# High and low weight parts in turn: the order of matmuls in block products and memory projections

## The chip, the cores and the metric

The kernel runs on one core of a Trainium2 chip. The metric is the device time of one execution in microseconds. An execution is described by five engines that each take their instructions in the order of the program: TensorE (PE in the profile, its weight loads apart as PEld), VectorE (DVE), ScalarE (ACT), GpSimd (POOL) and SyncE (SP), which issues most DMAs.

## The reference

One layer of a hybrid encoder for 512 tokens of width 2048, in float32:

```
y  = xn @ w_in                      # one input projection, xn = RMSNorm(x)
h += concat[GDN(y), RWKV7(y)] @ w_out
h += CrossAttn(RMSNorm(h), RMSNorm(mem)) :
     q = hn @ wq ; k = mn @ wk ; v = mn @ wv     # 256 memory tokens, 4 heads
     p = softmax(q k^T * XA_HEAD_DIM ** -0.5) ; (p v) @ wo
h += square(relu(hn @ mlp_w_up)) @ mlp_w_down    # hidden width 8192
out = RMSNorm_final(h)
```

The weights and the vectors are float32. The products of the kernel work on parts in a shorter format: a value is split into a high part, which is the value rounded, and a low part, which is what the rounding left.

## The kernel before, in words

**Stages.** PE goes through the following stages: 0 to 926 us, input projections (`py`) with the two mixers between them; 926 to 1036, the memory's key projections (`kp`), among the last of the mixers' work; 1036 to 1125, `kq`, a product of the query weights with the keys; 1125 to 1217, the memory's value projections (`vp`); 1217 to 1302, `vo`; 1302 to 1460, the out-projection as block products (`op`); 1460 to 1639, attention; 1639 to 2277, the first MLP matrix as block products (`up`); 2277 to 2897, the second.

**High and low.** A block of weights of 128x1024 is loaded by DMA (tiles `wr`, `ua`, `ub`), ACT casts it to its high part `whi` (line 130, 1.05 us), and DVE subtracts to get the low part `wlo` (line 131, 1.22 us); `split` issues both. The activations are split too; a tile of 128x512 holds the high part in its first 256 columns (`HA`) and the low part in the other 256 (`HB`). So a matmul of `whi` with all 512 columns forms high x high and high x low, and a matmul of `wlo` with the first 256 columns forms low x high. Both add to the same PSUM bank.

**Block products.** `op` has 8 steps p and `up` has 32, each with seven products on 2x2 blocks: B11 to bank x, T1 to y, T2 added on x, B21 to z, T3 added on x, B22 added on y, T4 added on x. After B11, T2 and T3 the bank x is read before the next product adds to it: ACT copies 256 columns into a tile `sl` and DVE adds the other 256 (after T3, DVE alone adds both). The weights of T1 and T2 are sums (`s1`) that DVE forms; those of T3 and B22 are sums too. At p = 0 of each stage the products go through `block`, at the others through `wide` (lines 1314 to 1321): eight high matmuls over k = 0..7, then eight low ones. There are 7 x 7 + 31 x 7 = 266 wide products. The activations' tiles are `cb0` (B11), `cb1` (T1), `cb2` (T2), `cb3` (T3), `cb4` (T4), `cb5` (B22) and `cb6` (B21).

**Buffers.** `whi` and `wlo` rotate over three buffers each (two in one pool, one in another), one step per product. So the cast of a product waits until the product three places earlier has read its high part for the last time; the buffer of B22 is that of T2.

**Memory projections.** `kp` (lines 546 to 552) and `vp` (lines 1354 to 1365) add up 16 blocks k for each of 16 output blocks. Both take the low matmul of a block before its high one, except at the first block of an output (`vp`: of each half), which starts with the high one. `kq` takes high, then low, all through. In the profile, all operations of the planned region up to `kq` carry line 228, and those of `vp`, `vo` and attention line 122, those of the helpers that issue them.

**What sets the order.** Up to `kq` the order is that of a plan in the program, which steps through generators. Behind it the code is issued through a tile framework, whose scheduler puts the instructions of each engine into an order of its own; the order of the code is not kept where data do not force it. PE then takes its rows strictly in the order that results.

Of the kernel before, what the change touches and what calls it, by code (L numbers as in the profile page):

```python
# [19 lines left out]
M = 256  # L20
KD = 16
# [52 lines left out]
def build(tc, I, out):  # L74
# [43 lines left out]
    def psb(nm, tag="mx", bufs=2):  # L118
        return tile_of(ps, [P, 512], F32, tag, nm, bufs)

    def mm(o, l, r, start=True, stop=True):
        PE.matmul(o, l, r, start=start, stop=stop)  # L122
# [59 lines left out]
    DV, AC, GS, TE, SY = (Lane(e, k) for e, k in ((V, "DVE"), (S, "ACT"), (GP, "POOL"), (PE, "PE"), (nc.sync, "SP")))  # L182
# [67 lines left out]
    def chain(gen, rank, done=None):  # L250
        chains.append([gen, rank, done, None, None])

    def after(*ev):
        return lambda: ev in events
# [63 lines left out]
    def act_tile(nm, dt=F32R):  # L318
        return tile_of(pa, [P, 512], dt, "act", nm, 32)
# [101 lines left out]
    def half(i):  # L421
        return lambda: i in halves and (i not in piece or ("piece", i) in events)
# [57 lines left out]
    def evict(n, pt):  # L480
        yield after("rstd")
        yield lambda: bool(yfree)
        b = yfree.pop(0)
        if n == 2:
            y = ybuf[b][0:64, 3:515]
            yield AC.copy(y, pt[64:128, :])
            yield DV.tensor_tensor(out=y, in0=pt[0:64, :], in1=y, op=ALU.add)
            yield DV.tensor_tensor(out=y, in0=y, in1=rstd[0:64, :], op=ALU.mult)
        else:
            yield DV.tensor_tensor(out=ybuf[b][:, 3:515], in0=pt, in1=rstd, op=ALU.mult)  # L490
        ys[n] = b
        events.add(("py", n))

    def gemm_(pts, his, los, first, nk=KD, left=None):

        w = len(pts)
        for h in range(nk // 8):
            for j in range(w):
                yield half(first + h * w + j)
            for kk in range(8):  # L500
                k = h * 8 + kk
                sl = slice(kk * P, (kk + 1) * P)
                yield lambda: len(his) > k
                if kk == 4:
                    yield lambda: all(first + h * w + j in whole for j in range(w))
                for j, pt in enumerate(pts):
                    wh, wl = halves[first + h * w + j]
                    yield TE.matmul(pt, wh[:, sl], his[k], start=(k == 0), stop=False)
                    yield TE.matmul(pt, wh[:, sl], los[k], start=False, stop=first == 4 and k == nk - 1)
                    if first != 4:  # L510
                        yield TE.matmul(pt, wl[:, sl], his[k], start=False, stop=(k == nk - 1))
                if left:
                    events.add((left, k))
            for j in range(w):
                used.add(first + h * w + j)
# [3 lines left out]
    def projections():  # L519
        pts = [psb(f"py{n}") for n in range(2)]  # L520
        yield from gemm_(pts, xhi, xlo, 0)
        for n in range(2):
            chain(evict(n, pts[n]), 0)
        for n in range(2, NIN):
            if n == NSQ[3] + 3:
                yield after("macc")
                pt = psb("pms", "mm", 2)
                mc = ybuf[macc[0]]
                yield TE.matmul(pt[:, 0:M], ones, mc[:, 0:M], start=True, stop=False)
                yield TE.matmul(pt[:, 0:M], ones, mc[:, M:2 * M], start=False, stop=True)  # L530
                chain(memnorm(pt, mc[:, M:2 * M]), 1)
            if n >= 4:
                yield after("py", n - 2)
            pt = psb(f"py{n}", "mm", 2)
            yield from gemm_([pt], xhi, xlo, 2 * n, left="x" if n == NIN - 1 else None)
            chain(evict(n, pt), 0)
        yield after("py", NIN - 2)
        kpt = {}
        for i, (n, h) in enumerate(kpo):
            if h == 0:  # L540
                yield after("kr", n - 2) if n >= 2 else after("py", NIN - 1)
                kpt[n] = psb(f"kp{n}", "mm", 2)
            pt = kpt[n]
            yield half(NKP + i)
            wh, wl = halves[NKP + i]
            for k in range(8 * h, 8 * h + 8):
                yield lambda: len(mhl) > k
                sl = slice(k % 8 * P, k % 8 * P + P)
                ab = [TE.matmul(pt, wh[:, sl], mhl[k], start=k == 0, stop=k == KD - 1),
                      TE.matmul(pt[:, 0:M], wl[:, sl], mhl[k][:, 0:M], start=False, stop=False)]  # L550
                yield from (ab if k == 0 else ab[::-1])
            used.add(NKP + i)
            if h == 0:
                continue
            khl.append(act_tile(f"khl{n}"))
            chain(kevict(n, pt, khl[n][:, 0:M], khl[n][:, M:2 * M]), 0)
        for i in range(2 * KD):
            n, g = i // 2, i % 2
            yield after("kp", KD - 2 + i) if i < 2 else after("kq", i - 2)
            yield half(NKQ + i)  # L560
            wh, wl = halves[NKQ + i]
            if i == 0:
                yield after("gated")
            pts = [psb(f"kq{n}_{g}_{hh}", t, 2) for hh, t in enumerate(("mm", "mg"))]
            for hh, o in enumerate(pts):
                for d in range(4):
                    k = g * 8 + hh * 4 + d
                    sl = slice((hh * 4 + d) * P, (hh * 4 + d + 1) * P)
                    yield TE.matmul(o, wh[:, sl], khl[k], start=(d == 0), stop=False)
                    yield TE.matmul(o[:, 0:M], wl[:, sl], khl[k][:, 0:M], start=False, stop=(d == 3))  # L570
            used.add(NKQ + i)
            chain(qevict(i, pts), 0)
# [590 lines left out]
    mhl = []  # L1163
# [26 lines left out]
    def memnorm(pt, mw):  # L1190
        yield from rsq_(mw, pt[:, 0:M], 1.0 / 2048, b_eps6)
        events.add(("mrs",))
        yield lambda: all(("py", i) in events for i in range(NIN))
        yield AC.copy(mrs, mw)
        events.add(("mrs", 1))
# [38 lines left out]
    def hilo():  # L1234
        cnt[0] += 1
        return (third("whi", f"whi{cnt[0]}", F32R, pw, NWS, "split", 1), third("wlo", f"wlo{cnt[0]}", F32R, pw, NWS, "split", 0))
# [78 lines left out]
    def wide(pt, a, parts, start):  # L1315
        hi, lo = hilo()
        split(a, hi, lo)
        for k in range(8):
            PE.matmul(pt, hi[:, k * P:k * P + P], parts[k], start=start and k == 0, stop=False, skip_group_check=True)  # L1319
        for k in range(8):  # L1320
            PE.matmul(pt[:, HA], lo[:, k * P:k * P + P], parts[k][:, HA], start=False, stop=k == 7, skip_group_check=True)  # L1321

    def block_or_wide(p, pt, a, parts, start):
# [28 lines left out]
    for n2 in range(8):  # L1352
        hi, lo = act_tile(f"vhi{n2}"), act_tile(f"vlo{n2}")
        for i in range(2):
            n = 2 * n2 + i
            pt = psb(f"vp{n}", "mm", 2)
            for h in range(2):
                wh, wl = wload(I["wv"][n][:, h * 1024:(h + 1) * 1024])
                for k in range(h * 8, h * 8 + 8):
                    sl = slice(k % 8 * P, k % 8 * P + P)  # L1360
                    if k == 0:
                        mm(pt, wh[:, sl], mhl[k], start=True, stop=False)
                    mm(pt[:, 0:M], wl[:, sl], mhl[k][:, 0:M], start=False, stop=False)
                    if k > 0:
                        mm(pt, wh[:, sl], mhl[k], start=False, stop=k == KD - 1)
            h2, l2 = hi[:, i * M:(i + 1) * M], lo[:, i * M:(i + 1) * M]
            u, t = rstd[:, M:2 * M], sl2(M)
            S.copy(u, pt[:, M:2 * M])
            V.tensor_tensor(out=t, in0=pt[:, 0:M], in1=u, op=ALU.add)
            V.tensor_tensor(out=t, in0=t, in1=mrs, op=ALU.mult)  # L1370
            split(t, h2, l2)
            vhi.append(h2)
            vlo.append(l2)
            mixes(1 + n % 2)
    for h in range(4):
        for g in range(4):
            pts = [psb(f"vo{g}_{h}_{mt}", ("mm", "mg")[g % 2]) for mt in range(2)]
            for q in range(2):
                wh, wl = wload(I["wo"][g, h][:, q * 1024:(q + 1) * 1024])
                for mt in range(2):  # L1380
                    for e in range(2):
                        d = q * 2 + e
                        sl = slice(e * 512, e * 512 + 512)
# [119 lines left out]
    for g in range(2):  # L1503
        pts = [psb(f"sc{g}_{t}", *(("mm", 2), ("mm", 2), ("mg", 2), ("mg", 2), ("scr", 1), ("scg", 1), ("mm", 2), ("mm", 2))[4 * g + t]) for t in range(4)]
        for n2 in range(8):
# [4 lines left out]
            wh, wl = hilo()  # L1510
# [40 lines left out]
        if g == 1:  # L1551
            for n in (0, 1, 2):
                pt = psb(f"at{n}", "mg", 2) if n < 2 else psb(f"at{n}", "scr", 1)
                begun.append((pt, *wload(vo_of(n))))
                attend(*begun[n], range(4))
        for e in range(2):
            for mt in range(2):
                pt = psb(f"ptr{g}_{e}_{mt}")
# [92 lines left out]
    for n in range(KD):  # L1651
        if n < 3:
            pt = begun[n][0]
            attend(*begun[n], range(4, 8))
        else:
            pt = psb(f"at{n}", "mm", 2)
# [374 lines left out]
```

## Time and profile before

| | before |
|---|---|
| runs, median (lowest to highest) | 2899.75 us (2895.79 to 2900.2), 3 runs |
| the profiled execution's own time | 2898.35 us |
| its span in the trace | 2896.6 us |
| granted TensorE clock in it | 0.999 |

The span runs from the first to the last instruction in the trace; 1.75 us of the execution's time lie around it. The page has the busy time of each engine, a row of tenths over 40 slices of the span (72.4 us each), the chain of work that ended last, and groups of instructions. In the timeline, PE matmuls that follow one another are given as one row with a count, the time from the first start to the last end; the matmuls are pipelined, so that one of 128x512 has a duration of 0.39 us but the next starts 0.23 us behind it. In the chain a group of matmuls counts from start to the next start.

### The profile page before, as it was taken

What the parts mean: (1) busy time and instruction counts of PE and PEld (TensorE: products, weight loads), DVE (VectorE), ACT (ScalarE), POOL (GpSimd) and SP (SyncE); (2) the same over time, 40 slices, a digit from 0 to 9 for tenths busy, and PEclk for the clock granted to TensorE, in tenths of its full rate; (3) what the DMA queues carried; (4) which work ended last, traced back from release to release, by engine and by line L of the source; (5) the groups of instructions that cost most, each with busy time, mean ns of one, the idle gap of its engine ahead of it and who ended that gap; (6) DMA issues with size and microseconds to landing.
All of it is one profiled execution on the core that took longest, in us unless ns stands there. A gap on an engine that the chain in (4) does not pass through costs nothing.

```text
span 2896.6 us, 48156 instructions
## 1 busy us (share of the span) xinstructions
PE 2870.5 (99%) x18458; PEld 2408.6 (83%) x18458; DVE 2223.9 (77%) x3379; ACT 1561.9 (54%) x2256; POOL 310.2 (11%) x704
## 2 busy tenths in 40 slices
PE   9999999999999999999999999999999999999998
PEld 7787787887877888889888888888888878888887
DVE  7676676676676767769866898888998897878776
ACT  7544554554546555664455555555555655454444
POOL 0302213113113000001111100010010000000000
PEclk9999999999999999999999999999999999999999
DMA  5333333424334579797788767788777988776765
GB/s 193 100 89 85 99 90 86 105 69 100 105 98 137 159 243 298 267 308 199 205 218 209 195 194 219 229 234 248 214 206 207 288 261 278 221 261 209 255 191 178
DMA packets 304503, 546.64 MB, mean 189 GB/s; under 512 B 97224, under 2 KB 178380, under 8 KB 303248
## 3 DMA queue, kind: packets, MB, share of 16 engines
q1 hardware_dynamic: 245264, 449.17, 49.3%
q0 software_dynamic: 35840, 67.12, 11.6%
q10 hardware_dynamic: 23168, 27.27, 2.6%
q8 instruction: 145, 2.38, 0.3%
q14 instruction: 86, 0.70, 0.1%
HBM read 479.10 MB, written 131.48 MB: 211 GB/s over the span
## 4 chain that ended last, share of the span: by engine, by line
PE 92%; DVE 3%; DMA 2%; POOL 1%; issue 1%; ACT 1%; SPq 0%; ACTq 0%; POOLq 0%; DVEq 0%
PE py L228 20%; PE upx L1319 8%; PE upx L1321 4%; PE upy L1319 4%; PE dx L1786 4%; PE dx L1785 4%; PE dx L1788 4%; PE vp L122 3%; PE kq L228 3%; PE sc L122 3%; PE at L122 3%; PE kp L228 3%; PE vo L122 3%; PE upy L1321 2%; PE upz L1319 2%; PE opx L1319 2%
## 5 line engine op out<-in xcount | busy, mean ns | idle before, releaser
L130 ACT CAST whi<-ub 128x1024 fp32r<-128x1024 f32 x290 | 304.5, 1052 | 274.1 <-PE dy L1786 59.0
L131 DVE TENSOR_TENSOR wlo<-ub,whi 128x1024 fp32r<-128x1024 f32 x290 | 352.6, 1220 | 60.5 <-ACT whi L130 55.1
L228 PE MATMUL py<-xhi,whi 128*128 128x512 f32 x928 | 371.0, 400 | 6.3 <-ACT xhi L228 6.3
L228 PE MATMUL py<-xlo,whi 128*128 128x512 f32 x928 | 372.1, 401 | 0.0
L228 PE MATMUL py<-xhi,wlo 128*128 128x512 f32 x912 | 370.9, 407 | 0.0
L228 ACT CAST whi<-wraw 128x1024 fp32r<-128x1024 f32 (+1 forms) x180 | 187.3, 1041 | 260.9 <-PE py L228 162.1
L130 ACT CAST whi<-ua 128x1024 fp32r<-128x1024 f32 x205 | 215.5, 1051 | 191.3 <-PE dx L1786 62.3
L131 DVE TENSOR_TENSOR wlo<-ua,whi 128x1024 fp32r<-128x1024 f32 x205 | 249.7, 1220 | 52.6 <-ACT whi L130 51.8
L228 DVE TENSOR_TENSOR wlo<-wraw,whi 128x1024 fp32r<-128x1024 f32 (+1 forms) x178 | 223.2, 1254 | 70.5 <-ACT whi L228 68.1
L1319 PE MATMUL upx<-cb,whi 128*128 128x512 f32 x992 | 249.8, 394 | 0.7 <-DVE sl L1277 0.7
L228 PEld LDWEIGHTS py<-xhi,whi 128*128 128x128 f32 x928 | 175.3, 189 | 40.6 <-ACT xhi L228 6.6
L228 PEld LDWEIGHTS py<-xlo,whi 128*128 128x128 f32 x928 | 174.9, 189 | 38.3 <-DVE xlo L228 1.0
L1319 PEld LDWEIGHTS upx<-cb,whi 128*128 128x128 f32 x992 | 178.5, 189 | 33.0 <-DVE sl L1277 0.9
L228 PEld LDWEIGHTS py<-xhi,wlo 128*128 128x128 f32 x912 | 172.4, 189 | 32.7 <-issue 1.0
L1785 PE MATMUL dx<-whi,dh 128*128 128x512 f32 x480 | 186.7, 389 | 0.0
L1786 PE MATMUL dx<-whi,dl 128*128 128x512 f32 x480 | 186.7, 389 | 0.0
L1321 PEld LDWEIGHTS upx<-cb,wlo 128*128 128x128 f32 x992 | 135.3, 190 | 9.7
L1321 PE MATMUL upx<-cb,wlo 128*128 128x256 f32 x992 | 138.3, 282 | 0.0
L131 DVE TENSOR_TENSOR wlo<-wr,whi 128x1024 fp32r<-128x1024 f32 x80 | 97.7, 1223 | 43.5 <-ACT whi L130 42.4
L1788 PE MATMUL dx<-wlo,dh 128*128 128x512 f32 x480 | 128.6, 389 | 0.0
L228 ACT ACT_TABLE_LOAD x86 | 110.3, 1283 | 26.2 <-DVE suml_gn L228 11.6
L1319 PE MATMUL upy<-cb,whi 128*128 128x512 f32 x496 | 124.3, 392 | 0.0
(898 smaller groups left out, 6676.2 us busy)
## 6 DMA issues: line engine op xcount, KB each, us to landing
ws<-in_w_dn POOLq DMA_DIRECT2D x128, 512.0 KB, 7.2
wraw<-in_w_in SPq DMA_DIRECT2D x116, 512.0 KB, 3.8
ua<-in_w_dn SPq DMA_DIRECT2D x108, 512.0 KB, 4.5
ub<-in_w_up SPq DMA_DIRECT2D x71, 512.0 KB, 6.3
ua<-in_w_up SPq DMA_DIRECT2D x56, 512.0 KB, 4.7
ub<-in_w_dn SPq DMA_DIRECT2D x52, 512.0 KB, 4.7
sl<-cd SPq DMA_DIRECT2D x104, 256.0 KB, 5.0
ub<-ws SPq DMA_DIRECT2D x52, 512.0 KB, 4.2
```

The lines of the kernel that those rows point to most:

```text
L122: PE.matmul(o, l, r, start=start, stop=stop)
L130: tie(S.copy(hi, src))
L131: V.tensor_tensor(out=lo, in0=src, in1=hi.bitcast(F32), op=ALU.subtract)
L228: f(*a, **k)
L1319: PE.matmul(pt, hi[:, k * P:k * P + P], parts[k], start=start and k == 0, stop=False, skip_group_check=True)
L1321: PE.matmul(pt[:, HA], lo[:, k * P:k * P + P], parts[k][:, HA], start=False, stop=k == 7, skip_group_check=True)
L1785: PE.matmul(pts[t], uh[:, x], hi[:, w], start=start and z == 0 and q == 0, stop=False, skip_group_check=True)
L1786: PE.matmul(pts[t], ul[:, x], hi[:, w], start=False, stop=False, skip_group_check=True)
L1788: PE.matmul(pts[t], uh[:, x], lo[:, w], start=False, stop=z == 1 and q == 3, skip_group_check=True)
```

## The change

In three places the high and the low matmul of a block now follow one another: in `wide` one loop issues both for each k, and in `kp` and `vp` the high one always comes first. Number, shapes and operands of the matmuls are as before.

```diff
@@ kp, line 546 @@
             for k in range(8 * h, 8 * h + 8):
                 yield lambda: len(mhl) > k
                 sl = slice(k % 8 * P, k % 8 * P + P)
-                ab = [TE.matmul(pt, wh[:, sl], mhl[k], start=k == 0, stop=k == KD - 1),
-                      TE.matmul(pt[:, 0:M], wl[:, sl], mhl[k][:, 0:M], start=False, stop=False)]
-                yield from (ab if k == 0 else ab[::-1])
+                yield TE.matmul(pt, wh[:, sl], mhl[k], start=k == 0, stop=False)
+                yield TE.matmul(pt[:, 0:M], wl[:, sl], mhl[k][:, 0:M], start=False, stop=k == KD - 1)
@@ wide, line 1317 @@
         for k in range(8):
             PE.matmul(pt, hi[:, k * P:k * P + P], parts[k], start=start and k == 0, stop=False, skip_group_check=True)
-        for k in range(8):
             PE.matmul(pt[:, HA], lo[:, k * P:k * P + P], parts[k][:, HA], start=False, stop=k == 7, skip_group_check=True)
@@ vp, line 1358 @@
                 for k in range(h * 8, h * 8 + 8):
                     sl = slice(k % 8 * P, k % 8 * P + P)
-                    if k == 0:
-                        mm(pt, wh[:, sl], mhl[k], start=True, stop=False)
-                    mm(pt[:, 0:M], wl[:, sl], mhl[k][:, 0:M], start=False, stop=False)
-                    if k > 0:
-                        mm(pt, wh[:, sl], mhl[k], start=False, stop=k == KD - 1)
+                    mm(pt, wh[:, sl], mhl[k], start=k == 0, stop=False)
+                    mm(pt[:, 0:M], wl[:, sl], mhl[k][:, 0:M], start=False, stop=k == KD - 1)
```

What the scheduler makes of it, at p = 8 of `up`. The rows are line, operation, tile written, tiles read, and shape; the number behind `up` is p, that behind `cb` is the set and then k. The high matmul's line is 1319 before and 1318 after, the low one's 1321 and 1319.

PE before, at the end of T3 (`cb3`), where B22 (`cb5`) begins:

```order
L1321 MATMUL upx8_18888<-cb3_6_16550,wlo1039_18986 128x256
L1321 MATMUL upx8_18888<-cb3_7_17227,wlo1039_18986 128x256
L1319 MATMUL upy8_18889<-cb5_0_16558,whi1040_19007 128x512
L1319 MATMUL upy8_18889<-cb5_1_16559,whi1040_19007 128x512
L1319 MATMUL upy8_18889<-cb5_2_16560,whi1040_19007 128x512
L1319 MATMUL upy8_18889<-cb5_3_16561,whi1040_19007 128x512
```

PE after, at the end of B21 (`cb6`), which here stands before T3:

```order
L1318 MATMUL upz8_18890<-cb6_7_17230,whi1038_18962 128x512
L1319 MATMUL upz8_18890<-cb6_7_17230,wlo1038_18963 128x256
L1318 MATMUL upy8_18889<-cb5_0_16558,whi1040_19007 128x512
L1319 MATMUL upy8_18889<-cb5_0_16558,wlo1040_19008 128x256
L1318 MATMUL upy8_18889<-cb5_1_16559,whi1040_19007 128x512
L1319 MATMUL upy8_18889<-cb5_1_16559,wlo1040_19008 128x256
L1318 MATMUL upx8_18888<-cb3_0_16544,whi1039_18985 128x512
L1319 MATMUL upx8_18888<-cb3_0_16544,wlo1039_18986 128x256
```

Before, the products followed one another whole: T1, T2, B21, T3, B22, T4. After, eight matmuls of B21 stand before T2 and eight behind it, then four of B22, then T3, then B22's other twelve. The same pattern stands at p = 8, 11, 14, 15 and 18; at p = 22, 27, 28 and 29 it is nine and seven of B21. At the other p these products stay whole or are cut by one or two rows; where rows of B22 stand ahead of T3 there (p = 1, 4 and 25), fourteen or fifteen of B21 stand between T2 and them.

PE after, a little later, at the end of B22, where T4 (`cb4`) begins:

```order
L1318 MATMUL upy8_18889<-cb5_7_17229,whi1040_19007 128x512
L1319 MATMUL upy8_18889<-cb5_7_17229,wlo1040_19008 128x256
L1318 MATMUL upx9_19086<-cb0_0_16523,whi1044_19091 128x512
L1318 MATMUL upx8_18888<-cb4_0_16551,whi1041_19031 128x512
L1319 MATMUL upx8_18888<-cb4_0_16551,wlo1041_19032 128x256
```

The first high matmul of B11 of p = 9 (`upx9`) stands ahead of T4 of p = 8, and the rest of that B11 behind it. One to four rows of the next p's B11 stand there at 23 of the p. Before, that happened at p = 4, 10, 11, 17, 18, 24 and 31 alone, with one to three rows.

DVE before, ahead of T2 of p = 8, with B11's eviction `sl1033` as the last row (`wlo1037` is the low part for T2, `wlo1038` for B21):

```order
L1277 TENSOR_TENSOR sl1025_18694<-sl1025_18694,upx7_18690 128x256
L131 TENSOR_TENSOR wlo1037_18940<-ub85_18887,whi1037_18939 128x1024
L131 TENSOR_TENSOR wlo1038_18963<-ub84_18885,whi1038_18962 128x1024
L1274 TENSOR_TENSOR sl1024_18693<-sl1024_18693,sl1025_18694 128x256
L1277 TENSOR_TENSOR sl1033_18891<-sl1033_18891,upx8_18888 128x256
```

DVE after, at the same place:

```order
L131 TENSOR_TENSOR wlo1037_18940<-ub85_18887,whi1037_18939 128x1024
L1273 TENSOR_TENSOR sl1024_18693<-sl1024_18693,sl1025_18694 128x256
L1273 TENSOR_TENSOR tt7_18857<-sl1024_18693 128x256
L1273 TENSOR_TENSOR t4_7_18858<-sl1025_18694,tt7_18857 128x256
L131 TENSOR_TENSOR wlo1038_18963<-ub84_18885,whi1038_18962 128x1024
L1276 TENSOR_TENSOR ub84_18885<-ub84_18885,ub85_18887 128x1024
L1276 TENSOR_TENSOR sl1033_18891<-sl1033_18891,upx8_18888 128x256
```

B11's eviction moved behind the 128x1024 addition into `ub84`, which stood behind it before.

## The prediction

> **What bounds the kernel now.** I read the page first: the busy shares, and then the chain that ended last.
>
> ```profile
> PE 2870.5 (99%) x18458; PEld 2408.6 (83%) x18458; DVE 2223.9 (77%) x3379; ACT 1561.9 (54%) x2256; POOL 310.2 (11%) x704
> ...
> DVE  7676676676676767769866898888998897878776
> ...
> PE 92%; DVE 3%; DMA 2%; POOL 1%; issue 1%; ACT 1%; SPq 0%; ACTq 0%; POOLq 0%; DVEq 0%
> ```
>
> TensorE is busy for 99% of the span and carries 92% of the chain. So the time is decided by two things only: how fast PE steps from one matmul to the next, and whether it ever waits. In the stages that the change touches, the chain of waits (out-projection block products, 1323 to 1459 us; then a closer window) is a plain row of products without a gap:
>
> ```profile
> 1323.19 1.84 PE opx L1319 x8
> ...
> 1330.62 0.95 PE opx L1321 x8
> 1331.57 1.84 PE opz L1319 x8
> 1333.41 0.95 PE opz L1321 x8
> 1334.36 1.84 PE opx L1319 x8
> ...
> 1373.47 1.84 PE opx L1319 x8
> ```
>
> Eight high matmuls take 1.84 us, eight low ones 0.95 us. From the first row to the last lie 18 products, (1373.47 - 1323.19) / 18 = **2.793 us a product**, 349.2 ns for a high and low pair. The list of PE's waits from 1300 to 2290 us, which holds out-projection, attention and MLP up, says that almost nothing else happens there:
>
> ```profile
> PE upx L1310 <- ACT whi L130: 0.8, 1, 0.8
> PE upx L1319 <- DVE sl L1277: 0.7, 1, 0.7
> PE at L122 <- ACT phi L1562: 0.2, 1, 0.2
> ```
>
> The columns are the total, the number of waits and the longest: 1.7 us in all. A gain from removed waits is therefore not to be had in these stages. The change can win only by a faster step, and it can lose both by a slower step and by new waits.
>
> **The change, part by part.** Number and shapes of the matmuls, the casts, the subtractions and the DMAs stay. Only PE's order is written anew; the other engines' order follows from the scheduler.
>
> *1. The step of a pair in turn.* Two stages of before already alternate 128x512 high with 128x256 low matmuls, and the chain gives a row of each:
>
> ```profile
> 1036.24 87.95 PE kq L228 x507
> ...
> 1125.00 90.25 PE vp L122 x512
> ```
>
> `kq` takes high, low, high, low without a break: 87.95 / 507 x 2 = 346.9 ns a pair. `vp` takes low before high, but its first pair of each product the other way round, so that once per product two high and then two low ones meet: 90.25 / 512 x 2 = 352.5 ns. Grouped, the wide products take 349.2, between the two. So the same matmuls cost -1% or +1% by how they follow each other. The timeline of `vp` shows that the break costs more than its own place:
>
> ```profile
> 1142.38 0.28 PE L122 MATMUL vp<-mhl,wlo 128*128 128x256 f32 x1
> 1142.50 0.40 PE L122 MATMUL vp<-mhl,whi 128*128 128x512 f32 x1
> 1142.74 0.28 PE L122 MATMUL vp<-mhl,wlo 128*128 128x256 f32 x1
> 1142.86 0.40 PE L122 MATMUL vp<-mhl,whi 128*128 128x512 f32 x1
> 1143.10 0.28 PE L122 MATMUL vp<-mhl,wlo 128*128 128x256 f32 x1
> 1143.21 0.40 PE L122 MATMUL vp<-mhl,whi 128*128 128x512 f32 x1
> 1143.44 0.28 PE L122 MATMUL vp<-mhl,wlo 128*128 128x256 f32 x1
> ```
>
> From start to start: 0.12, 0.24, 0.12, 0.24, 0.11, 0.23. High steps of 0.24 stand between some of 0.23, far from any break; the slow sequence goes on over the product, as a state that one break sets. The rate in the changed products then hangs on whether they are broken. By the new order of PE they mostly are: one to four rows of the next p's B11 are set ahead of T4 of the p before at 23 places of the MLP, an odd number at 16 of them, so that two high and later two low ones meet, and other products are cut in two. Wholly unbroken are p = 2 and 3 of the MLP and p = 1, 2, 4, 5 of the out-projection: 6 x 7 = 42 of the 266 wide products. I take the rate of `kq` for these, 8 x 0.3469 = 2.775 us: 42 x -0.018 = -0.8 us; and that of `vp` for the other 224, 8 x 0.3525 = 2.820: 224 x +0.027 = +6.0. **Together +5.2 us.** The two ends are all at the rate of `kq`, 266 x -0.018 = -4.8, and all at that of `vp`, +7.2. I lean to the slow end since a break's state lasted in the only stage that shows breaks.
>
> The Trainium skill, page "TensorE: Matmul & The Clock Gate", section "Back-to-back issue gap", gives a gap per matmul that hangs on its columns alone, 216 ns for 512 and by the same formula an estimated 109 ns for 256. By it a pair would take 325 ns in any order, and this term would be nothing. The rows speak against it: no stage here goes below 346.9, and the same pair took 346.9 or 352.5 in two orders.
>
> *2. `vp` and `kp`.* `vp` becomes unbroken, since its products stay whole: 256 pairs x (346.9 - 352.5) ns = **-1.4 us** (if its state is inherited, 0). `kp` is woven among the last mixer work, so its pieces are short, at about 347 ns a pair already (the longest: 16.91 / 94 x 2 = 360 with other work inside, a shorter one 3.47 / 20 x 2 = 347); I take 0 within 1 us either way.
>
> ```profile
> 953.90 3.47 PE kp L228 x20
> ...
> 1019.10 16.91 PE kp L228 x94
> ```
>
> *3. The weight buffer comes free later.* The high parts rotate over three buffers, so a product's cast on ACT waits for the last high matmul three products earlier. Grouped, that is the 8th of 16 matmuls, in turn the 15th: 7 low ones or 7 x 0.12 = 0.83 us later. For whole products this is hidden. Here is p = 16 (T2 at 1967.83, B22 at 1976.21, whose buffer is that of T2):
>
> ```profile
> 1965.28 0.37 ACT L1594 COPY sl<-upx 128x256 f32<-128x256 f32 x1
> 1966.36 0.41 DVE L1277 TENSOR_TENSOR sl<-sl,upx 128x256 f32<-128x256 f32 x1
> 1967.83 2.00 PE L1319 MATMUL upx<-cb,whi 128*128 128x512 f32 x8
> ...
> 1971.10 1.05 ACT L130 CAST whi<-ub 128x1024 fp32r<-128x1024 f32 x1
> 1971.57 2.36 DVE L131 TENSOR_TENSOR wlo<-ub,whi 128x1024 fp32r<-128x1024 f32 x2
> ...
> 1973.42 2.00 PE L1319 MATMUL upx<-cb,whi 128*128 128x512 f32 x8
> ...
> 1975.26 1.11 PE L1321 MATMUL upx<-cb,wlo 128*128 128x256 f32 x8
> 1975.50 1.05 ACT L130 CAST whi<-ub 128x1024 fp32r<-128x1024 f32 x1 [1.74 <-PE upx L1319]
> 1976.21 2.00 PE L1319 MATMUL upy<-cb,whi 128*128 128x512 f32 x8
> 1977.11 1.22 DVE L131 TENSOR_TENSOR wlo<-ub,whi 128x1024 fp32r<-128x1024 f32 x1
> ```
>
> The cast for B22 ran at 1971.10 and its low part was done at about 1973.9, 2.3 us ahead of B22. A release 0.83 us later leaves 1.5 us.
>
> *4. B22 begun ahead of T3: the new wait.* But the new order doesn't keep that lead. In nine p of the MLP (8, 11, 14, 15, 18, 22, 27, 28, 29) two pairs of B22 stand before T3, right behind the second half of B21, which itself follows T2 (its first half stands ahead of T2). PE takes its rows in order, so it arrives at B22's first low matmul a whole product sooner, just when the buffer's release is late. From the start of T2's last high matmul the low part takes: its 0.23 us; 0.24 to the cast (its high matmuls ended 1.84 us after 1973.42, and the cast that waited for them began at 1975.50); cast 1.05; subtraction 1.22 (rows above); and about 0.17 to PE's steady step again, from the one wait that the trace has:
>
> ```profile
> 1767.32 0.41 DVE L1277 TENSOR_TENSOR sl<-sl,upx 128x256 f32<-128x256 f32 x1
> ...
> 1767.79 0.96 PE L1319 MATMUL upx<-cb,whi 128*128 128x512 f32 x3 [0.66 <-DVE sl L1277]
> ```
>
> (0.06 from the end of the addition, 1767.73, to PE; three matmuls took 0.96, where three at 0.23 and the 0.16 of the last one's drain, 2.00 - 1.84, would take 0.85: 0.11.) Sum 2.91 us. In that time PE has left to do: that last high matmul 0.23, its low one 0.12, eight matmuls of B21 at 0.347 a pair, 1.39, and B22's first high matmul 0.23: 1.97 us in five of the nine p; in the other four (22, 27, 28, 29) seven of B21, 1.16: 1.74 us. The wait is 0.94 x 5 + 1.17 x 4 = **9.4 us**. Behind the waiting matmul PE's whole queue stands, so all of it counts. Its bounds: 0 if the scheduler's order leaves ACT and DVE ahead in a way that the rows hide, which three buffers exclude for the cast; and where DVE has another 1.22 us addition or subtraction before it in its queue, 9 x 1.22 = 11 more. I keep the sum of the rows.
>
> *5. T2's wait for B11's eviction.* T2 accumulates on the bank of B11, so it waits for ACT's copy and DVE's addition (1965.28 and 1966.36 above, where 1.1 us were to spare before T2). In the new order DVE has a 128x1024 addition of about 1.22 us ahead of this small one, and in the p where B21 is begun first, T2 comes 1.39 us later. The push and the cover nearly cancel; in about ten p some wait is left. Bounds: 0, and ten times the one measured wait of this kind, 0.66, so 6.6. I take 0.2 each, **2.0 us**, nearer to 0 since the push is covered in whole where the order is cut in eights.
>
> **Sum:** +5.2 - 1.4 + 9.4 + 2.0 = +15.2 us on the profiled run's 2898.35: 2913.6. The median of the runs is 1.4 above that profiled run, less than their spread of 4.4, so I forecast **2914 us**, 0.5% slower.
>
> **The rivals.**
>
> (a) *Waits as priced, but the breaks set no state.* All 266 products then go at the rate of `kq`: -4.8 - 1.4 + 9.4 + 2.0 = +5.2, 2904. For it: in the new order only one pair in about 56 is out of turn, while in `vp` it is one in 16. Against it: the sequence in `vp` did not recover within its 15 other pairs.
>
> (b) *Faster.* The low parts of B22 are in place when PE gets there, T2 finds its addition done, and the steady turn wins as in `kq`: -4.8 - 1.4, 2892. It hangs on one thing, the wait at B22's first low matmul in those nine p: were it under 0.47 us each, half of what I price, with the rate of `kq`, the sum would turn below zero. For it: whole products have leads of microseconds (the 2.3 above). Against it: the release itself lies within 2 us of the use, and cast plus subtraction alone take 2.27.
>
> (c) *Nothing happens.* Order does not matter to PE and the waits are hidden: 2898. By the Trainium skill's gap per matmul (section named above) that would be so for term 1; rows of two rates speak against that, and the wait is independent of it.
>
> (d) *Slower still.* DVE, whose slices in the MLP (22 to 31 of the row of tenths above) are at 8 and 9 tenths already, falls behind, and its queue puts one 1.22 us operation before half of the waited-for subtractions and T2's addition comes later: 9.4 + 5 + 6 + 7.2 = +27.6, 2926.
>
> **How the numbers follow.** Forecast (with its own spread of 2909 to 2920) 0.55; (a) 0.20; (b) 0.06; (c) 0.07; (d) 0.12. A measurement of this kernel can tell about 0.2%, 5.8 us, from no change. (a) lies just inside that; half of it counts as same: same 0.07 + 0.10 = 0.17; faster 0.06; slower 0.77. The range leaves out (b) and most of (c), and the far part of (d): 2900 to 2926.
>
> **What would show it.** In the list of PE's waits, nine new ones on DVE's `wlo` at `upy`, of about 1 us, in those p, and none in the others; some short ones on `sl` at `upx`. In the chain of waits, `vp` at about 88.8 us instead of 90.25. In stretches of the MLP without a wait a pair of 352 ns if I am right, 347 if (a) is. The forecast is wrong if PE's waits between 1640 and 2280 us sum to under 4 us, or if the pair's step leaves the two rates that before shows.

## The result, and the profile after

| | before | after |
|---|---|---|
| median (lowest to highest) | 2896.51 us (2895.79 to 2900.20) | 2912.53 us (2908.83 to 2917.78) |
| ratio to before, 95% interval | | 1.0052 [1.0042, 1.0062] |
| the profiled execution, its span | 2898.35, 2896.6 us | 2913.96, 2912.2 us |

The kernel is 16 us slower. (The kernel before has six runs here, the three shown ahead of the prediction and three more, so its median is lower than the one there.) From the starts of the stages in the two traces, the 15.6 us of the spans come from: 1.6 before the out-projection (of which 1.35 lie ahead of the first matmul), 4.1 in the out-projection, nothing in attention (179.65 and 179.67 us), 9.95 from the start of the MLP to the end. Taken apart at the last matmul of MLP up, MLP up is 11.7 us longer and what follows it 1.7 us shorter.

The page's first part, and the one group among its costliest in which PE's matmuls waited:

```profile
PE 2878.0 (99%) x18458; PEld 2406.6 (83%) x18458; DVE 2236.6 (77%) x3379; ACT 1564.7 (54%) x2256; POOL 312.7 (11%) x704
...
L1319 PE MATMUL upy<-cb,wlo 128*128 128x256 f32 x496 | 140.0, 282 | 6.3 <-DVE wlo L131 6.3
```

PE's busy time rose by 7.5 us only, though the matmuls are the same; the busy share cannot show what happened, the waits can. The list of waits of the weight loads shows more than that of the matmuls (a matmul that starts late behind its weights isn't idle in the other list). The columns are the total, the number, the longest. Before, the only wait on `sl` for DVE in the two stages is this one, in MLP up:

```profile
PEld upx L1319 <- DVE sl L1277: 0.9, 1, 0.9
```

After, in the out-projection (first row) and MLP up:

```profile
PEld opx L1318 <- DVE sl L1276: 3.5, 8, 2.2
...
PEld upy L1319 <- DVE wlo L131: 9.1, 9, 1.1
PEld upx L1318 <- DVE sl L1276: 2.8, 10, 0.5
PEld upx L1309 <- ACT whi L130: 1.0, 1, 1.0
PEld upy L1318 <- ACT whi L130: 0.7, 4, 0.2
PEld upx L1319 <- DVE wlo L131: 0.2, 1, 0.2
```

The nine waits at B22 are there, 9.1 us. The waits on `sl` are those for evictions of bank x, 6.3 us: 3.5 in 14 steps at T2, and 2.8 in four at T3, 2.2 of it at one step of the out-projection. One of the nine in the timeline (p = 29; ACT, DVE and weight loads):

```profile
2243.78 1.05 ACT L130 CAST whi<-ub 128x1024 fp32r<-128x1024 f32 x1 [3.05 <-PE upx L1318]
...
2244.87 1.23 DVE L131 TENSOR_TENSOR wlo<-ub,whi 128x1024 fp32r<-128x1024 f32 x1 [2.63 <-ACT whi L130]
...
2244.89 0.19 PEld L1318 LDWEIGHTS upy<-cb,whi 128*128 128x128 f32 x1 [0.18 <-ACT whi L130]
2246.15 0.19 PEld L1319 LDWEIGHTS upy<-cb,wlo 128*128 128x128 f32 x1 [1.07 <-DVE wlo L131]
```

The cast waits for T2's last high matmul (`upx`), the subtraction for the cast, and B22's first low matmul for the subtraction. DVE had been idle for 2.63 us: it was not short of time, it had nothing released.

The chain of waits around the memory projections, after:

```profile
1036.35 54.95 PE kq L228 x317
...
1126.14 90.45 PE vp L122 x512
```

`vp` takes 90.45 us where 88.8 were forecast; `kq` steps with 54.95 / 317 x 2 = 346.7 ns a pair up to 1091 us, and behind a wait at 1100 us, by the starts of its matmuls, with 353.

### The profile page after: what moved, and what is told of

It is laid out like the page before. It is cut to its first block, busy times and chain, and to the rows that moved or that the text cites. A ratio compares the mean times of both kernels' runs of the same rounds, so it can differ in the third digit from the quotient of the medians.

```text
span 2912.2 us, 48153 instructions
## 1 busy us (share of the span) xinstructions
PE 2878.0 (99%) x18458; PEld 2406.6 (83%) x18458; DVE 2236.6 (77%) x3379; ACT 1564.7 (54%) x2256; POOL 312.7 (11%) x704
## 4 chain that ended last, share of the span: by engine, by line
PE 65%; DVE 2%; ACT 1%; DMA 1%; issue 0%; ACTq 0%; DVEq 0%; SPq 0%
PE upx L1318 8%; PE upx L1319 4%; PE upy L1318 4%; PE dx L1781 4%; PE dx L1783 4%; PE dx L1780 4%; PE vp L122 3%; PE sc L122 3%; PE at L122 3%; PE vo L122 3%; PE kp L228 3%; PE kq L228 3%; PE upy L1319 2%; PE dy L1780 2%; PE dy L1781 2%; PE dy L1783 2%
## 5 line engine op out<-in xcount | busy, mean ns | idle before, releaser
L1318 PE MATMUL upx<-cb,whi 128*128 128x512 f32 x992 | 352.2, 397 | 0.3
L1319 PE MATMUL upx<-cb,wlo 128*128 128x256 f32 x992 | 278.6, 281 | 0.0
L1318 PEld LDWEIGHTS upx<-cb,whi 128*128 128x128 f32 x992 | 185.5, 188 | 44.8 <-DVE sl L1276 2.8
L1319 PEld LDWEIGHTS upx<-cb,wlo 128*128 128x128 f32 x992 | 187.5, 189 | 0.9 <-DVE wlo L131 0.2
L1318 PE MATMUL upy<-cb,whi 128*128 128x512 f32 x496 | 177.6, 396 | 0.0
L1319 PE MATMUL upy<-cb,wlo 128*128 128x256 f32 x496 | 140.0, 282 | 6.3 <-DVE wlo L131 6.3
```

## The experiments

Ratios are to the kernel before on the same chip. The theory after the result was: the time comes from the new order, above all from B22 ahead of T3, and products kept whole would bring it back. The rival: the turn itself costs, since each buffer comes free 0.83 us later, and the order is only the scheduler's answer to that.

### Which part, and products kept whole

**e_wide** and **e_proj** hold one part of the change each: `wide` alone, or `kp` and `vp` alone.

> Only the wide block products take high and low in turn; kp and vp stay as before. My theory (the time comes from waits that the new order of the block products brings, most of all B22's low part where two pairs of B22 stand before T3): ratio to before 1.004 to 1.0065, nine PE waits of 0.8 to 1.0 us on DVE wlo at upy in MLP up, some 3 us on DVE sl at opx and upx. Rival (the memory projections carry it): within 0.2% of before.

Measured: 1.0058 [1.0045, 1.0070], 9.1 us in nine waits at `upy`, 5.7 us on `sl`. The wide products carry all of it.

> Only kp and vp change; the wide products are as before. My theory: within 0.2% of before, and vp's rate is set by which of two steps (347 or 353 ns a pair) it comes into, not by its own order: 88.8 or 90.4 us for vp. The recorded prediction's step: vp falls to 88.8 us, -1.4 us in all. Rival (the memory projections carry it): ratio about 1.005.

Measured: 1.0000 [0.9991, 1.0008]. `vp` fell to 88.75 us in the chain of waits:

```profile
1127.45 88.75 PE vp L122 x512
```

So the same order of `vp` took 90.45 us after the change and 88.75 here.

**e_kept** pins the first and the last matmul of each wide product behind what stands ahead of it in the code, so that all products are whole:

```diff
         for k in range(8):
-            PE.matmul(pt, hi[:, ...], parts[k], ...)
-            PE.matmul(pt[:, HA], lo[:, ...], parts[k][:, HA], ...)
+            op = PE.matmul(pt, hi[:, ...], parts[k], ...)
+            if k == 0:
+                tc.keep_in_program_order(op)
+            op = PE.matmul(pt[:, HA], lo[:, ...], parts[k][:, HA], ...)
+            if k == 7:
+                tc.keep_in_program_order(op)
```

> High and low in turn as after the change, but each wide product's first and last matmul are kept in the order of the code, so all 266 stand whole: T1, T2, B21, T3, B22, T4. My theory: the nine waits on wlo at upy are gone and those on sl are under 1 us, and what is left is the step alone, between -5 us (347 ns a pair all through) and +9 us (353.5): ratio 0.998 to 1.003, likeliest 1.000. Rival (the turn itself costs, since the high part's buffer comes free 0.83 us later for every product): waits on wlo at many products, ratio 1.004 or more.

Measured: 1.0063 [1.0050, 1.0076]. The nine waits are gone and the kernel is no faster: my theory fell. Its weight loads wait for evictions instead (out-projection, then MLP up):

```profile
PEld opx L1318 <- DVE sl L1276: 4.5, 12, 1.5
...
PEld upx L1318 <- DVE sl L1276: 9.3, 8, 1.9
PEld upx L1318 <- issue: 6.6, 23, 0.5
```

**e_keptb** is the same pin with the grouped products of before.

> The kernel before, grouped, with the same two matmuls of each wide product kept in the order of the code as in the other runs: DVE's order is as before, and the few rows of B11 that stood before T4 are put back. Every theory: within 0.2% of before, no new waits; if keeping the order itself costs something, the ratio is above 1.002 and the runs with kept products are to be read against this one.

Measured: 1.0011 [1.0002, 1.0020], with two waits on `sl` of 2.6 us in all near the start of the MLP. Against this kernel e_kept is still half a per cent slower, so the pins are not its cause.

**e_b22** pins only T3's last and B22's first matmul.

> As after the change, but only the last matmul of T3 and the first of B22 are kept in the order of the code, so B22 never stands before T3; T2 and B21 are still cut into each other. My theory: the nine waits on wlo at upy (9.1 us of weight loads) are gone, those on sl before T2 (about 3 us in up) stay; ratio 1.001 to 1.003. Rival (B22's waits only moved: what waits for the late cast then waits at T3 or T4): the sum of PE's waits stays near 9 us and the ratio at 1.005.

Measured: 1.0127 [1.0112, 1.0143]. The waits at B22 are down to one, 1.0 us, but T2 and B21 are now cut into each other at 18 steps, and T3 waits for T2's eviction, up to 1.8 us a step (28.3 of the 32.0 us below; the rest is at T2):

```profile
PEld upx L1318 <- DVE sl L1276: 32.0, 37, 1.8
```

Both theories missed: the wait moved, and grew. What the four kernels with the wide products in turn have in common (the one after the change, e_wide, e_kept, e_b22) are waits for evictions of bank x, additions on DVE. I turned to DVE's order.

### DVE's order, first attempts

**e_fours** takes four high, four low, four high, four low, with whole products; only the order of the 16 matmuls in `wide` differs from e_kept:

```diff
-        for k in range(8):
+        for j, (low, k) in enumerate([(l, 4 * h + k) for h in (0, 1) for l in (0, 1) for k in range(4)]):
```

> Whole products, four high, four low, four high, four low, so the high part is read for the last time in the 12th of 16 matmuls: 0.48 us later than before, where in turn it is 0.83. In this kernel's order DVE has two 128x1024 operations between T2's low part and B11's eviction at 22 steps of up; with whole products in turn there were 5. Theory (DVE's order sets T2's wait): about 22 waits of 1.2 to 1.9 us on sl before T2, ratio 1.009 to 1.015, and hardly a wait at T4 since the release is 0.35 us earlier. Rival (the release alone sets it): fewer waits than with whole products in turn, ratio 1.000 to 1.005.

Measured: 1.0134 [1.0120, 1.0148], and T2's waits as counted from DVE's order:

```profile
PEld upx L1321 <- DVE sl L1276: 33.4, 23, 1.9
```

T4's waits, 23 rows of "issue" in e_kept, are gone. That fits the earlier release, but DVE's order differs here too. So two things may decide: where the eviction stands in DVE's queue, and when the buffer comes free.

**e_evict** and **e_best** were to put evictions ahead with the same kind of pin:

```diff
+            tc.keep_in_program_order(V.tensor_tensor(out=c1[:, HA], in0=c1[:, HA], in1=x[:, HB], op=ALU.add))
...
+            tc.keep_in_program_order(V.tensor_tensor(out=a12, in0=a12, in1=s1, op=ALU.add))
```

> As the run with whole products in turn, and on DVE B11's eviction (the addition that T2 waits for) is also kept ahead of the 128x1024 addition that forms B22's weights. Theory now (DVE's order: where that addition stands ahead of the eviction, T2 waits 1.9 us): T2's waits on sl in up fall from 9.3 to under 1.5 us, those of T4 behind B22 (0.2 to 0.3 each) stay, ratio to before 1.002 to 1.004. Rival (the later release of the buffers holds DVE back whatever its order is): T2's waits stay, ratio 1.006.

> As e_evict, and DVE also takes T3's second eviction, which T4 waits for, ahead of the low part of the next step's B11, whose cast waits for T3's buffer. Theory: T4's waits go too (in up some 6 us of weight loads), no wait on sl or wlo over 0.2 us is left in the wide products but in the first steps, and what is left is the step alone: 347 or 353.5 ns a pair against 349.2 before, ratio 0.998 to 1.002. Rival (late release): waits come back at other products, ratio 1.003 or more.

Measured: 1.0305 [1.0291, 1.0319] and 1.1194 [1.1179, 1.1210]. They test nothing that I meant: a pin sets an instruction behind the one ahead of it on its engine in the code, and for the addition of B22's weights that is B21's second eviction. B22's weights were then formed only after B21 had ended, and in MLP up B22 waited at 30 steps (40.0 us on `wlo`, 21.4 on `whi`); in e_best B11 waited there 163 us on low parts besides. All they show is how little room DVE's queue has: in e_evict one operation put a product too late costs 2 us a step.

### The two orders, with and without the turn

Now the whole order of PE, DVE and ACT, from the out-projection's p = 1 to the end of MLP up, was held by a table of edges, each instruction behind the one ahead of it in that order (no wait, issue order only):

```diff
+def as_before(tc):
+    at = {i.name: i for i in tc.nc.cur_bb.bb.instructions}
+    for step in json.loads(zlib.decompress(base64.b85decode(ORDER))).values():
+        n, last = 0, None
+        for d in step:
+            n += d
+            i = at[f"I-{n}"]
+            if last is not None:
+                tc.add_manual_dep(i, last.name, mybir.DependencyInfo(mybir.DependencyClass.NoSync, ...), ...)
+            last = i
```

> Wide products in turn (kp and vp as before), but from the out-projection's p = 1 to the end of MLP up the instructions of PE, DVE and ACT are held in the order of the kernel before, product by product. So only what the turn itself does is left: the step, and buffers that come free 0.83 us later. If the new order alone costs the time: within 0.2% of before. If the late release alone does: 1.005 or more, with waits at many products. What I expect from the traces: before, T3's second eviction was done 0.7 us ahead of T4, and it stands behind a low part whose cast waits for the release; so T4 waits 0.1 to 0.3 us in most steps, 4 to 9 us in all, T2 and B22 hardly at all: ratio 1.001 to 1.004.

> The reverse: wide products grouped as before (eight high, eight low), but PE, DVE and ACT held, over the same stretch, in the order that the scheduler makes for products in turn, with T2 and B21 cut into each other and four matmuls of B22 ahead of T3 (here four high ones). If the new order alone costs the time: ratio 1.003 to 1.005. If it costs only together with the late release: within 0.2% of before, the nine waits on wlo at upy gone, since the cast is released 0.83 us earlier and no low matmul of B22 stands ahead of T3; at T2 up to 3 us of waits on sl.

| | orders of before | orders made for the turn |
|---|---|---|
| grouped | before: 1 | e_cross: 1.0036 [1.0022, 1.0050] |
| in turn | e_same: 1.0086 [1.0072, 1.0100] | e_wide: 1.0058 [1.0045, 1.0070] |

In turn with the orders of before is the slowest of the four. The turn costs 0.86% by itself; the new order, which alone costs 0.36%, takes back 0.28 of it. No run holds the grouped kernel in its own order by such a table, so what the table alone costs isn't measured; e_swap2 below, whose table is as long, bounds it at 0.33%. The waits at B22 on `wlo` are gone in e_cross, as expected. Its waits on `sl` in MLP up are 8.0 us in 17: T2 has 2.5 of them, where up to 3 were expected, but T3 has 4.4 and T4 1.1, which weren't. In e_same such waits stand at most steps:

```profile
PEld opx L1335 <- DVE sl L1293: 2.3, 10, 0.6
PEld opx L1335 <- issue: 1.5, 7, 0.3
...
PEld upx L1335 <- DVE sl L1293: 12.1, 33, 0.6
PEld upx L1335 <- issue: 6.6, 22, 0.4
```

That is 22.5 us, where before had 0.9; the two stages are 23.3 us longer than before. At T4 it is 8.1 us, inside the 4 to 9 that I had expected; the 11.1 at T2 and 3.3 at T3 I hadn't. The timelines show how T2 gets there. Before, around the end of B11 (a step near 2083 us):

```profile
2082.29 1.12 PE L1321 MATMUL upx<-cb,wlo 128*128 128x256 f32 x8
2082.71 1.04 ACT L130 CAST whi<-ub 128x1024 fp32r<-128x1024 f32 x1
2083.78 1.23 DVE L131 TENSOR_TENSOR wlo<-ub,whi 128x1024 fp32r<-128x1024 f32 x1 [0.25 <-ACT whi L130]
2084.18 0.35 ACT L1594 COPY sl<-upx 128x256 f32<-128x256 f32 x1
2085.26 0.41 DVE L1277 TENSOR_TENSOR sl<-sl,upx 128x256 f32<-128x256 f32 x1
2086.03 2.00 PE L1319 MATMUL upx<-cb,whi 128*128 128x512 f32 x8
```

and in e_same:

```profile
2082.68 0.40 PE L1335 MATMUL upx<-cb,whi 128*128 128x512 f32 x1
2082.91 0.28 PE L1336 MATMUL upx<-cb,wlo 128*128 128x256 f32 x1
2083.11 1.05 ACT L146 CAST whi<-ua 128x1024 fp32r<-128x1024 f32 x1
2084.20 1.23 DVE L147 TENSOR_TENSOR wlo<-ua,whi 128x1024 fp32r<-128x1024 f32 x1 [0.41 <-ACT whi L146]
2084.60 0.35 ACT L1609 COPY sl<-upx 128x256 f32<-128x256 f32 x1
2085.68 0.41 DVE L1293 TENSOR_TENSOR sl<-sl,upx 128x256 f32<-128x256 f32 x1
2086.14 0.19 PEld L1335 LDWEIGHTS upx<-cb,whi 128*128 128x128 f32 x1 [0.45 <-DVE sl L1293]
```

The cast and the `wlo` are those of B21, whose buffer is B11's. B11's last high matmul has streamed at 2082.29 before and at 2082.91 in e_same; cast and subtraction follow, DVE stands idle for the cast, and **B11's eviction stands behind that subtraction in DVE's queue**. All that the eviction itself waits for is ACT's copy of the other columns, done at 2084.95 in e_same, 0.73 us before the eviction starts. T2 needs the eviction. Before, it was done at 2085.67, 0.36 us ahead of T2 and 2.43 behind T1's first matmul (2083.24); in turn it is done 3.06 us behind T1's first matmul (2083.03), 0.63 later, and T2 waits. T4's wait is the same chain: T3's second eviction stands behind the low part of the next B11, which has T3's buffer. In e_kept:

```profile
1779.40 1.23 DVE L131 TENSOR_TENSOR wlo<-ua,whi 128x1024 fp32r<-128x1024 f32 x1 [0.19 <-ACT whi L130]
1780.54 0.41 DVE L1276 TENSOR_TENSOR sl<-sl,upx 128x256 f32<-128x256 f32 x1
1781.07 0.19 PEld L1318 LDWEIGHTS upx<-cb,whi 128*128 128x128 f32 x1 [0.27 <-issue]
```

The profile names no releaser for T4's load ("issue"), but the eviction ended 0.12 us ahead of it.

### Undoing the chain

**e_swap** is e_same with B11's eviction moved, in the table for DVE, ahead of B21's low part, and T3's ahead of the next B11's. **e_swap2** moves T2's as well, ahead of B22's.

> As e_same (in turn, orders of the kernel before), with two moves in DVE's order at each step: B11's eviction ahead of B21's low part (30 steps), T3's second eviction ahead of the next B11's low part (36 steps). Theory: T2 waits because B11's eviction stands behind the low part of B21, whose cast waits for B11's last high matmul, and T4 likewise behind T3; with both moved, the waits on sl (22 us in e_same) fall under 4 us and the step alone is left, 347 to 353.5 ns a pair: ratio 0.998 to 1.003. Rival (DVE as a whole is too late, whatever stands first): the waits move to wlo at upz and upy and the ratio stays at 1.006 or more.

Measured: 1.0058 [1.0044, 1.0071]. T2 and T4 hardly wait in MLP up any more. At the same step as above, B11's eviction now stands ahead of the low part and waits for ACT's copy alone:

```profile
2076.75 0.42 DVE L1293 TENSOR_TENSOR sl<-sl,upx 128x256 f32<-128x256 f32 x1 [1.03 <-ACT sl L1609]
2077.09 1.22 DVE L147 TENSOR_TENSOR wlo<-ua,whi 128x1024 fp32r<-128x1024 f32 x1
```

It is done at 2077.17, 2.37 us behind T1's first matmul (2074.80), where e_same has 3.06, and 0.46 ahead of T2 (2077.63). But T3 waits at 24 steps of MLP up and five of the out-projection, 14.3 us in all, on T2's eviction, which stands behind the low part of B22, whose buffer is T2's:

```profile
2081.96 1.22 DVE L147 TENSOR_TENSOR wlo<-ua,whi 128x1024 fp32r<-128x1024 f32 x1
2083.09 0.42 DVE L1293 TENSOR_TENSOR sl<-sl,upx 128x256 f32<-128x256 f32 x1
2083.56 0.19 PEld L1335 LDWEIGHTS upx<-cb,whi 128*128 128x128 f32 x1 [0.44 <-DVE sl L1293]
```

The ratio missed what I expected, since more than half of the waits had only moved one product on.

> As e_swap, and T2's eviction, too, ahead of B22's low part, whose cast waits for T2's last high matmul (19 more moves). In e_swap T2 and T4 no longer waited; T3 did, 0.4 to 0.6 us at 20 steps, behind just that. Theory (each x eviction must stand ahead of the low part that waits for the same product's last high matmul): the waits on sl fall from 14 us to under 4, no other waits come, and what is left is the step, 347 or 353.5 ns a pair: ratio 0.999 to 1.003. Rival (DVE is too late in all): they move on, ratio 1.005.

Measured: 1.0033 [1.0021, 1.0045], and in the MLP

```profile
PEld upx L1335 <- DVE sl L1293: 4.6, 10, 0.5
```

Both are a little over what I expected (waits under 4 us, at most 1.003). From 1.0086 to 1.0058 to 1.0033, by 85 moves of one small addition each on DVE and nothing else in the orders that are held: the tables of the three kernels for PE and ACT are the same. That shows the mechanism. What is left of 9.6 us are about 5 us of waits and the step of the pair: in the MLP 352.3 ns, from the starts of its matmuls (steps with a wait left out), against 349.2 before, (352.3 - 349.2) x 1736 pairs = 5.4 us. None of the kernels beats the one before.

## Why the prediction was right, and where it was not

The time, 2914 for 2912.5 measured, and the sign were right. Of the terms, the waits at B22, the waits at T2 and the nothing for `kp` were right; the step and `vp` were not, the waits at T3 were not in the sum, and one reason was wrong.

*The nine waits at B22* (9.4 us): right in place, number and size. 9.1 us were measured. They come in two sizes as worked out, 0.9 (five times) and 1.13 us (four times) of lost time per step (from the starts: 0.80 and 1.03 at the high matmul, 0.1 at the next), for 0.94 and 1.17 forecast.

*T2's wait for B11's eviction* (2.0 us, bounds 0 and 6.6): near enough. T2's waits on `sl` are 3.5 us in both stages; 0.9 were there before, so 2.6 are new. What the sum lacks is T3, which waits for T2's eviction in the same way: 2.8 us. Together 5.4 are new.

*The step in turn* (+5.2 us, 84% of the products slow): the two rates are right, and so is that a rate lasts once it is set, but what sets it is not. From the starts, the mean pair after is 351.8 ns in the out-projection and 349.8 in the MLP, against 349.2: 2.6 ns x 392 pairs + 0.6 ns x 1736 pairs = about 2.1 us. Cuts are not needed for the slower rate nor do they force it (last section).

*`vp`* (-1.4): it came out at +0.2, since it came in at the slower rate; in e_proj it was -1.5. The step "unbroken, so at the rate of `kq`" failed: `vp` takes whichever of the two rates it comes into. I had noted that alternative in brackets and priced it rightly.

*The buffer that comes free later, "for whole products this is hidden"*: **this step failed.** I followed the late release through one product's own cast and subtraction, found 1.5 us to spare at B22, and stopped there. I didn't follow what stands behind that subtraction in DVE's queue: the evictions of bank x, with 0.36 us to spare at T2. In turn with the orders of before, the step costs 21.6 us of new waits where I wrote 0. The total was spared this, because I had added it up for the order that the scheduler makes for the turn, and in that order other waits, the nine at B22 above all, stand in place of most of these. That the scheduler trades them on account of the later release is likely, but not shown.

So the reason "the new order brings the waits" is half of it: that order alone costs 0.36% and the turn without it 0.86%.

The forecast counted 15.2 us. By terms, after has: 9.1 + 0.9 (the other waits on `whi` and `wlo`) + 5.4 of waits, 2.1 + 0.2 for the steps, and -2.6 in MLP down, where the waits of weight loads fell from 3.3 to 0.7 us, which the prediction didn't look at. (It need not be the change's doing: in e_proj, where the block products are as before, they are 0.2.) Together 15.1, and 1.1 lie ahead of `vp`; the spans differ by 15.6. So the nearness of the two sums is in part luck: a step priced 3.1 us too high makes up for the waits at T3, and MLP down for most of what else is missing.

*The rivals.* (a) left the rate to `kq`: the rate was between. (b), faster, and (c), nothing, needed hidden waits; none was hidden. (d) put late evictions into DVE's load: they do come from DVE, but from its order behind released work, not from its load.

## What to carry to other kernels

When an instruction that frees a buffer moves later, follow the release past the operation that takes the buffer to everything that stands behind that operation in its engine's queue; the slack that counts is that of the last one which somebody waits for. An eviction that the next product needs shouldn't stand behind a conversion that waits for the same product's last read. And where a scheduler decides the order, its new order may be part of the cure as well as a cost of its own: hold the old order and try, before it is blamed.

## What the runs showed of the hardware that was not expected

Matmuls of 128x512 and 128x256 in turn run in one of two steady rhythms, for stretches of up to hundreds of pairs. In the timeline of `kq` after the change, both stand side by side:

```profile
1098.94 0.39 PE L228 MATMUL kq<-khl,whi 128*128 128x512 f32 x1
1099.17 0.27 PE L228 MATMUL kq<-khl,wlo 128*128 128x256 f32 x1
1099.28 0.40 PE L228 MATMUL kq<-khl,whi 128*128 128x512 f32 x1
...
1100.67 0.39 PE L228 MATMUL kq<-khl,wlo 128*128 128x256 f32 x1 [0.30 <-DVE wlo L228]
...
1101.24 0.40 PE L228 MATMUL kq<-khl,whi 128*128 128x512 f32 x1
1101.48 0.28 PE L228 MATMUL kq<-khl,wlo 128*128 128x256 f32 x1
1101.60 0.40 PE L228 MATMUL kq<-khl,whi 128*128 128x512 f32 x1
1101.84 0.28 PE L228 MATMUL kq<-khl,wlo 128*128 128x256 f32 x1
```

Ahead of the wait a high matmul takes 0.23 us to the next start, behind it 0.24. By starts the short rhythm is about 230 + 117 = 347 ns a pair and the long one repeats 233 117 241 120 236 113 ns, 353.3 a pair. The rhythm is carried across products and stages (`kq` into `vp`). It mostly changes at a wait or a cut, but not only: in e_kept and e_cross `kq` went from the long one to the short one 3 us after its start, with no step there above 242 ns. The same kind of wait left the short one at one step and the long one at another. In the seven kernels that have the new order of `vp`, it took 88.7 us in three profiled executions and 90.4 in four. In e_swap2 the whole out-projection but its start ran in the short one:

```profile
1352.53 0.39 PE L1335 MATMUL opz<-cm,whi 128*128 128x512 f32 x1
...
1449.60 0.39 PE L1335 MATMUL opz<-cm,whi 128*128 128x512 f32 x1
```

Five steps of seven products, (1449.60 - 1352.53) / 35 = 2.773 us a product, less than the 2.793 of grouped ones; the MLP of the same execution was mostly in the long one. So the turn would win 0.7% of a product in the one rhythm and lose 1.2% in the other, and nothing here shows what chooses. It may be part of why executions after the change spread over 9 us and before over 4.4; that wasn't tried.

The rule of the Trainium skill that the prediction weighed ("TensorE: Matmul & The Clock Gate", section "Back-to-back issue gap"), a gap that hangs on the columns alone, gives one rate for all of these, an estimated 325 ns a pair; no stage measured here is below 346.7. That section of the Trainium skill states the gap for an isolated matmul and says that in a stream the weight loads set the spacing too, so it was a weak rival.
